# Neighbourhood attention regrouped into blocks of 8 grid columns, and narrower end tiles in the window attention

## The chip, the cores and the metric

One core of one Trainium2 chip runs the whole program. The metric is the time of one execution in device microseconds (us); lower is better. Three runs of the kernel before gave 2230.81, 2233.44 and 2235.84 us, so the median is 2233.44 us.

## What is computed

A backbone of two layers over 512 latent tokens (a grid of 8 rows by 64 columns) and 256 context tokens, 1,024 channels wide, all in fp32. In each layer the normalised tokens are projected to queries, keys and values of four attention branches with four heads each: A (latent attention, dense), B (window: a latent query sees latent keys at a distance of at most 128), C (neighbourhood) and D (normalised queries and keys, dense). Every latent query also sees all 256 context keys in the same softmax. The context tokens see context keys alone, and only layer 0 needs them. Each branch's output is projected, multiplied by a gate (a sigmoid of a product of the tokens with a 1,024 x 1,024 matrix per branch) and summed; then come an output projection and a mixture of 32 experts.

The part that matters here, cut from the reference (8 grid rows, so a query sees all rows):

```python
c_start = clip(q_col - NA_KW // 2, 0, GRID_W - NA_KW)      # NA_KW = 16, GRID_W = 64
col_ok = (k_col >= c_start) & (k_col < c_start + NA_KW)
dc = clip(k_col - q_col, -(NA_KW - 1), NA_KW - 1) + NA_KW - 1
bias = rpb[:, dr, dc]                                      # dr: row distance; 0 for context keys
s = where(row_ok & col_ok, q @ k * scale + bias, -1e30)
```

So of the 512 latent keys a query of branch C sees 16 columns of 8 rows, 128 keys, and the rest is masked.

## The kernel before, in words

Tokens are handled in six tiles of 128: 0 to 3 latent (each two grid rows), 4 and 5 context. fp32 values are split in a high and a low part in the fast fp32 format ("fp32r"), and a product is three products (`mm3`, L306); `projT` (L664) makes 128 channels by up to 512 tokens in one PSUM bank, so 24 matmuls, and `proj` (L657) one token tile by 256 channels, also 24.

`branch_c` (L829) works in two halves of two heads. `qk` (L833) projects queries and keys in `projT` form, 512 latent tokens and then 256 context tokens; `val` (L853) projects the values one token tile at a time. `bias_c` (L1106) loads a table of 128 x 896 for each head through the POOL queue and combines it with the column mask on DVE.

`attend` (L1071) cuts a half into groups of 256 queries, two of them latent, and a group into four tiles (two query tiles by two heads). `scores` (L1114) makes one tile: the products of 128 queries with the latent keys (512, in branch B 384) and the 256 context keys into a PSUM buffer of two banks (`sps`, two of these); DVE takes the row minimum of the context part and adds the bias or the mask to the latent part while taking the minimum on (L1135, L1142); ACT takes the exponential with its sum (L1152); DVE scales (L1156, L1157); then PE transposes P in pieces of 128 keys into banks (`bk`, four of these, L256) and ACT copies them to `pt` (L1169). `values` (L1091) multiplies `pt` with the values in plain fp32, both heads side by side in the array, copies the sum (L1101) and writes it to DRAM on the SP queue (L1102).

The order on PE is written out by a planner, `Flow` (L143): it keeps a clock from an estimate for each matmul (`mat`, L244) and fixed latencies (the tables `LT`, one per layer) for the time until a buffer is free again or a result is ready. Where the attention's items are not ready, it puts in a filler, `gates` (L1173): the 32 gate products of the layer, with the products of the modulation vector between them in layer 0 (`mod_seg`, L392), whose weights come through the SP queue (L403, L285). Whatever is left of the filler runs on into `merge` (L1205), which reads the branch outputs back from DRAM (`load`, L1220). The other engines take their orders from the framework's scheduler. Expert weights are loaded on the SP queue (L1644) as buffer slots come free.

Of the kernel before, what the change touches and what calls it, by code (L numbers as in the profile page):

```python
# [9 lines left out]
F32 = mybir.dt.float32  # L10
# [3 lines left out]
AF = mybir.ActivationFunctionType  # L14
ALU = mybir.AluOpType
# [8 lines left out]
NL = 2  # L24
# [3 lines left out]
BIG = 1e30  # L28
# [17 lines left out]
def consts():  # L46
    c = {}
    c["ident"] = np.eye(128, dtype=np.float32)
    c["rope_h"] = _rope(SEQ, 64)
    c["rope_a"] = _rope(SEQ, 32)  # L50
    a, b = np.arange(128)[:, None], np.arange(128)[None, :]
    full = np.full((128, 128), BIG, np.float32)
    zero = np.zeros((128, 128), np.float32)
    lo = np.where(b >= a, 0.0, BIG).astype(np.float32)
    hi = np.where(b <= a, 0.0, BIG).astype(np.float32)
    c["bmask"] = np.concatenate([full, lo, zero, hi, full], 1)
    qc = np.arange(128)[:, None] % 64
    kc = np.arange(64)[None, :]
    cs = np.clip(qc - 8, 0, 48)
    c["cmask"] = np.where((kc >= cs) & (kc < cs + 16), 0.0, BIG).astype(np.float32)  # L60
# [24 lines left out]
def prep(x, c, ctx, c_ctx, w_mod, b_mod, g_norm_mix, w_in, g_q_a, w_q_b, g_kv_a, w_kv_b,  # L85
         sink_b, rpb_c, g_q_d, g_k_d, w_gate, b_gate, w_branch, w_out, g_norm_ffn,
         w_group, b_group, w_router, b_router, w_ff1, w_ff3, w_ff2, g_final):
    r = {}
# [26 lines left out]
    pad = np.zeros((NL, 4, 15, 128), np.float32)  # L115
    pad[..., 48:79] = rpb_c
    qc, kc = np.arange(64)[:, None], np.arange(64)[None, :]
    sk = pad[..., kc - qc + 63]
    bt = np.stack([sk[:, :, 1:15], sk[:, :, 0:14]], 2)
# [113 lines left out]
class Build:  # L233
# [110 lines left out]
    def setup(self):  # L344
# [12 lines left out]
        def rest():  # L357
            self.rope_h = ld("rope_h", [128, 4, 2, 64])
            self.rope_a = ld("rope_a", [128, 4, 2, 32])
            self.bmask = ld("bmask", [128, 640])  # L360
            self.cmask = ld("cmask", [128, 64])
            self.iota = ld("iota", [128, 64])
            self.trib = c.tile([128, 128], BF, name="trib")

# [299 lines left out]
    def projT(self, W, c0, t0, n):  # L664

        ps = self.bank()
        c = slice(c0, c0 + 128)
        self.mm3(ps[:, :n], [(W(0, k)[:, c], W(1, k)[:, c], self.hsl(0, k, t0, n), self.hsl(1, k, t0, n))
                             for k in range(8)])
        return ps  # L670

    def nop(self, give=0, fn=None):
# [156 lines left out]
    def branch_c(self):  # L829
# [3 lines left out]
        def qk(hb, part, t0, n):  # L833
# [3 lines left out]
            for j in range(2):  # L837
                own, oth = slice(64 * j, 64 * j + 64), slice(64 - 64 * j, 128 - 64 * j)
                if part == 0:
                    q = hf.q(t0, n)  # L840
                    nc.scalar.activation(q[own, j], ps[own, :n], AF.Copy, scale=-0.125)
                    nc.vector.scalar_tensor_tensor(q[oth, j], ps[own, :n], -0.125, q.bitcast(F32)[own, j],
                                                   op0=ALU.mult, op1=ALU.subtract)
# [9 lines left out]
        def val(t):  # L853
# [4 lines left out]
            return  # L858
            yield

        vals = []
        for hb in range(2):
            load, new = self.load_unit(box, 4 + 2 * hb), self.new_half(box, hb, "m")
            bias = f.item(self.nop(0, lambda hb=hb: box.__setitem__(("bt", hb), [self.bias_c(2 * hb + j)
                                                                                for j in range(2)])), slots=2)
            pre = [load, new, bias]
            ps = []
            for t0, n in ((0, 512), (512, 256)):
# [11 lines left out]
            out.append((pre, proj, lambda hb=hb, ps=ps: self.attend("c", 2, hb, box, ps + vals, None), 7))  # L880
        return out

    def head_norm(self, s, H):
# [184 lines left out]
        return out  # L1068


    def attend(self, br, n, hb, box, qs, ks):  # L1071


        f = self.fl
        items = []
        for g in range(3 if self.wc else 2):
            kts = [4, 5]
            if g < 2:
                kts = list(range(g, g + 3) if br == "b" else range(4)) + kts
            groups = [kts[i:i + 3] for i in range(0, len(kts), 3)]  # L1080
            PT = [[], []]
            tiles = []
            for qi in range(2):
                deps = qs if ks is None else [qs[2 * g + qi]] + [ks[t] for t in kts]
                for j in range(2):
                    tiles.append(f.item(self.scores(br, hb, box, j, g, qi, groups, PT[j]), deps=deps, lat=self.LT["evac"],
                                        need=("S", "P")))
            items += tiles + [f.item(self.values(n, hb, box, g, kts, PT), deps=tiles, lat=self.LT["pv"], need=("bk",))]
        return items

    def values(self, n, hb, box, g, kts, PT):  # L1091
        f, hf = self.fl, box[hb]
        acc = self.bank()
        f.use("bk", self.LT["oacc"])
        for i, kt in enumerate(kts):
            for j in range(2):
                self.mat(acc[64 * j:64 * j + 64, :256], hf.v(j, kt), PT[j][i // 3][:, i % 3, :],
                         start=i == 0, stop=i == len(kts) - 1, tile_position=(0, 64 * j))
        f.left["pt1"] += len(PT[0]) + len(PT[1])
        oT = self.t1("oT")  # L1100
        self.nc.vector.tensor_copy(oT, acc[:, :256])  # L1101
        self.nc.sync.dma_start(self.ob[n][hb][:, g * 256:(g + 1) * 256], oT)  # L1102
        return
        yield

    def bias_c(self, h):  # L1106
        nc = self.nc
        bt = self.slot(name="bt")[:, :896].rearrange("p (u c) -> p u c", u=14)
        nc.gpsimd.dma_start(bt.rearrange("p u c -> p (u c)"), self.a["rpb"][self.l, h])
        nc.vector.scalar_tensor_tensor(bt, bt, -1.0, self.cmask[:, None, :].to_broadcast([128, 14, 64]),  # L1110
                                       op0=ALU.mult, op1=ALU.add)
        return bt

    def scores(self, br, hb, box, j, g, qi, groups, PT):  # L1114
# [5 lines left out]
        q0 = g * 256 + qi * 128  # L1120
# [3 lines left out]
        q = hf.q(q0, 128)[:, j]  # L1124
        for c0, cn, kk in ([(lo, kn, k0)] if lat else []) + [(512, 256, 512)]:
            self.mat(S[:, c0:c0 + cn], q, hf.kh(0, j, kk, cn), start=True, stop=False)
            self.mat(S[:, c0:c0 + cn], q, hf.kh(1, j, kk, cn), start=False, stop=br != "a")
            if br == "a":
                self.mat(S[:, c0:c0 + cn], hf.qr(q0, 128)[:, j], self.KR[:, kk:kk + cn], start=False, stop=True)
        m = self.tiny.tile([128, 1], F32, name="m", tag="m", bufs=4)  # L1130
        if br in "ad" or not lat:
            nc.vector.tensor_reduce(m, S[:, lo:768], axis=AX.X, op=ALU.min)  # L1132
        else:
            m0 = self.tiny.tile([128, 1], F32, name="m0", tag="m0", bufs=4)
            nc.vector.tensor_reduce(m0, S[:, 512:768], axis=AX.X, op=ALU.min)  # L1135
            if br == "b":
                o = {0: 2, 1: 1, 2: 1, 3: 0}[2 * g + qi]
                bias = self.bmask[:, o * 128:o * 128 + 384]
            else:
                u = 7 - 2 * (2 * g + qi) - 1  # L1140
                bias = box["bt", hb][j][:, u:u + 8].rearrange("p u c -> p (u c)")
# [18 lines left out]
        for gi, grp in enumerate(groups):  # L1160
            if gi:
                yield 0.0, ("bk",)
            elif qi == 0:
                PT += [self.sm.tile([128, 3, 256], F32, name="pt", tag="pt", bufs=NPT) for _ in groups]
                f.left["pt1"] -= len(groups)
            w = len(grp)
            f.use("bk", self.LT["pt"])
            v = self.transposed([Pt[:, (gi * 3 + i) * 128:(gi * 3 + i + 1) * 128] for i in range(w)])
            nc.scalar.activation(PT[gi][:, :w, qi * 128:(qi + 1) * 128], v, AF.Copy)  # L1169
        f.left["P"] += 1  # L1170


# [843 lines left out]
```

## Time and profile before

| | |
|---|---|
| median of 3 runs | 2233.44 us (2230.81 to 2235.84) |
| the profiled execution | 2233.74 us, span 2232.0 us |
| PE busy | 2068.5 us (93% of the span) |
| DVE, ACT, POOL busy | 1288.5, 808.8, 295.7 us |
| mean granted clock of PE | 0.965 |
| DMA | 430.92 MB, 193 GB/s on average |

PE is TensorE's matmuls and PEld its weight loads, DVE is VectorE, ACT ScalarE, POOL GpSimd and SP the engine that issues most DMAs. A row of the timeline gives start, duration and, after the shape, how many instructions were merged in it; matmuls overlap, so the distance from start to start says what one costs PE, not its duration. "L251" is the helper through which nearly every matmul goes, "L256" the one for transposes. A matmul in plain fp32 shows as two rows.

### The profile page before, as it was taken

The numbers are of one execution on the slowest core, as the hardware profiler recorded it, in microseconds if no ns is written. First come the engines' busy times: TensorE is split into PE (matmuls) and PEld (weight loads), VectorE is DVE, ScalarE is ACT, GpSimd is POOL, SyncE is SP. The second block draws the span as 40 slices with busy tenths as digits, with TensorE's granted clock in tenths as the row PEclk, the third lists the DMA queues.
The fourth block names the chain that finished last, engine by engine and source line by source line (L and its number), as shares of the span: only waits on it lengthen the run. The fifth ranks groups of instructions, "written<-read, shape, count | busy, mean of one in ns | idle before, by whom it ended". The sixth has DMA issues, their size and how long they took to land. (4 is left out here: it accounts for less than half of the span.)

```text
span 2232.0 us, 34108 instructions
## 1 busy us (share of the span) xinstructions
PE 2068.5 (93%) x13005; PEld 1524.7 (68%) x13005; DVE 1288.5 (58%) x2655; ACT 808.8 (36%) x1817; POOL 295.7 (13%) x321
## 2 busy tenths in 40 slices
PE   5999999999999988969999979999999998699997
PEld 3878777777887877934444468877888787644443
DVE  4464454345544565677777766555466476746655
ACT  4454454344444221212222235565455432211112
POOL 1101100011100144230000031000020013200000
PEclk8999999999999998979999989999999999899999
DMA  7452443543223555679999423112212387699992
GB/s 280 144 195 95 152 155 113 171 149 119 81 78 115 188 187 197 227 254 402 365 366 364 178 76 107 55 48 90 90 46 86 121 259 263 226 379 407 406 406 80
DMA packets 141813, 430.92 MB, mean 193 GB/s; under 512 B 19344, under 2 KB 32032, under 8 KB 141648
## 3 DMA queue, kind: packets, MB, share of 16 engines
q1 hardware_dynamic: 127120, 388.36, 48.4%
q0 software_dynamic: 13088, 35.10, 4.8%
q10 hardware_dynamic: 1440, 5.24, 0.6%
q8 instruction: 104, 1.70, 0.3%
q14 instruction: 61, 0.50, 0.1%
HBM read 398.67 MB, written 36.78 MB: 195 GB/s over the span
## 5 line engine op out<-in xcount | busy, mean ns | idle before, releaser
L251 PE MATMUL bk<-hT,wH 128*128 128x512 f32 (+1 forms) x1760 | 480.2, 360 | 2.8 <-ACT wH L275 2.1
L251 PEld LDWEIGHTS bk<-hT,wH 128*128 128x128 f32 x1760 | 300.1, 189 | 51.4 <-issue 8.1
L251 PE MATMUL bk<-hT,wL 128*128 128x512 f32 (+1 forms) x880 | 311.8, 354 | 7.6 <-DVE wL L276 7.6
L1786 DVE TENSOR_TENSOR x<-x,sps 128x1024 f32<-128x1024 f32 x166 | 195.5, 1216 | 101.0 <-PE sps L1785 100.6
L1727 PE MATMUL bk<-e,xT 128*64 128x512 f32 x1056 | 245.8, 603 | 0.0
L251 PE MATMUL bk<-wH,hT 128*128 128x256 f32 x1248 | 240.5, 287 | 1.3 <-DVE sk L276 1.0
L251 PEld LDWEIGHTS bk<-wH,hT 128*128 128x128 f32 x1248 | 200.0, 193 | 5.3 <-DVE sk L276 1.3
L251 PEld LDWEIGHTS bk<-hT,wL 128*128 128x128 f32 x880 | 166.3, 189 | 33.4 <-DVE wL L276 9.8
L275 ACT ACTIVATE wH<-wraw 128x1024 fp32r<-128x1024 f32 x132 | 139.1, 1058 | 125.1 <-DMA wraw<-in_w_gate_dram 41.5
L276 DVE TENSOR_TENSOR wL<-wraw,wH 128x1024 fp32r<-128x1024 f32 x112 | 138.8, 1245 | 70.2 <-ACT wH L275 39.4
L251 PE MATMUL bk<-wL,hT 128*128 128x256 f32 x624 | 177.2, 284 | 0.0
L1727 PEld LDWEIGHTS bk<-e,xT 128*64 128x64 f32 x1056 | 72.1, 138 | 142.9 <-issue 125.7
L1152 ACT ACTIVATE P<-sps,m 128x768 f32<-128x768 f32 (+2 forms) x160 | 126.5, 792 | 77.0 <-DVE m L1132 52.7
L1169 ACT ACTIVATE pt<-bk 128x384 f32<-128x384 f32 (+1 forms) x288 | 120.8, 467 | 74.7 <-PE bk L256 73.6
L1785 PE MATMUL sps<-yeH,to 128*128 128x512 f32 x332 | 142.7, 430 | 2.4 <-ACT yeH L275 1.4
L256 PE MATMUL bk<-ident,P 128*128 128x128 f32 x800 | 121.2, 282 | 19.2 <-ACT pt L1169 7.3
L1785 PE MATMUL sps<-yeL,to 128*128 128x512 f32 x332 | 132.2, 398 | 1.7 <-DVE yeL L276 1.7
L322 POOL TENSOR_TENSOR rr<-rs,mhalf 128x1 f32<-128x1 f32 (+1 forms) x72 | 52.3, 727 | 572.5 <-DVE rs L318 500.9
L1750 PE MATMUL bk<-e,gT 128*64 128x512 f32 x528 | 122.3, 606 | 1.5 <-ACT gT L1743 1.5
L256 PEld LDWEIGHTS bk<-ident,P 128*128 128x128 f32 x800 | 91.7, 142 | 46.7 <-ACT pt L1169 15.4
L251 PEld LDWEIGHTS bk<-wL,hT 128*128 128x128 f32 x624 | 120.3, 193 | 0.6
L1733 ACT ACTIVATE eth<-bk 128x256 f32<-128x256 f32 x33 | 12.7, 385 | 285.7 <-PE bk L1727 285.7
(355 smaller groups left out, 3671.4 us busy)
## 6 DMA issues: line engine op xcount, KB each, us to landing
e<-in_w_dram SPq DMA_DIRECT2D x384, 512.0 KB, 7.5
wmod<-in_w_mod_dram SPq DMA_DIRECT2D x96, 512.0 KB, 4.6
wraw<-in_w_gate_dram SPq DMA_DIRECT2D x64, 512.0 KB, 4.0
wraw<-in_w_in_dram SPq DMA_DIRECT2D x36, 512.0 KB, 4.9
thd<-th SPq DMA_DIRECT2D x64, 256.0 KB, 3.4
thm<-thd SPq DMA_DIRECT2D x32, 384.0 KB, 3.1
wraw<-in_w_br_dram SPq DMA_DIRECT2D x16, 512.0 KB, 4.0
wraw<-in_w_out_dram SPq DMA_DIRECT2D x16, 512.0 KB, 6.1
```

The lines of the kernel that those rows point to most:

```text
L251: return self.nc.tensor.matmul(out, lhsT, rhs, **kw)
L256: return self.nc.tensor.transpose(out, src, self.ident if ident is None else ident)
L275: nc.scalar.activation(H, src, AF.Copy)
L276: (eng or nc.vector).tensor_tensor(L, src, H.bitcast(F32), op=ALU.subtract)
L322: self.nc.gpsimd.tensor_tensor(r[:, :n], o[:, :n], self.mhalf.to_broadcast([128, n]), op=ALU.pow)
L1152: nc.scalar.activation(Pt[:, :n], S[:, lo:768], AF.Exp, scale=-1.0, bias=m, accum_out=sm)
L1169: nc.scalar.activation(PT[gi][:, :w, qi * 128:(qi + 1) * 128], v, AF.Copy)
L1727: nc.tensor.matmul(box["h"][64 * z:64 * z + 64, :], xT(k, z), W(z, k // 2)[:, (k % 2) * 512:(k % 2 + 1) * 512], start=k == 0, stop=k == 7, ...
L1733: nc.scalar.activation(th[s], H[s, :256], AF.Tanh, scale=0.5)
L1750: nc.tensor.matmul(Y[n][64 * z:64 * z + 64, :], gT[:, k, 64 * z:64 * z + 64], W(z, 4 + k)[:, n * 512:(n + 1) * 512], start=k == 0, stop=k ...
L1785: nc.tensor.matmul(ps[:, c], to[s, t * 128:(t + 1) * 128], w[s, c], start=i == 0, stop=i == 1)
L1786: nc.vector.tensor_tensor(self.x1[t] if out is None else out, self.x1[t], ps, op=ALU.add)
```

## The change

The 64 grid columns are cut into 8 blocks of 8; a block has 8 rows by 8 columns, 64 tokens. The q, k and v products of branch C's latent tokens are written to PSUM in block order (block, row, column) by a strided output pattern; the tokens are still read in their old order. The queries are copied out rotated by one block, so that the query tiles are blocks (1, 2), (3, 4), (5, 6) and (7, 0); the key tiles are blocks (0, 1), (2, 3), (4, 5), (6, 7). A query tile then sees two key tiles, 256 latent keys: tile u sees u and u + 1, the last one sees 0 and 3. The values of the latent tokens are projected as `projT` too (channels by tokens), copied and transposed back on PE. The bias with the mask in it comes as one table of 128 x 1,024 for a half (2 heads, 2 kinds of query tile, 256 keys) and is negated on ACT. In branch B the first and the last query tile see 256 latent keys in place of 384. `values` multiplies a key tile with the queries that see it alone, context tile 4 first and 5 last. The outputs of branch C are put back in grid order by four copies and written in pieces of 32, 24 or 8 columns.

```diff
 # prep
-    r["rpb"] = f(bt.transpose(0, 1, 2, 4, 3, 5).reshape(NL, 4, 128, 14 * 64))
+    for qb, kb in (((1, 2), (0, 1, 2, 3)), ((7, 0), (0, 1, 6, 7))):
...
+        tabs.append(np.where(ok, rpb_c[:, :, kr[None] - qr[:, None] + 7, dc], np.float32(-BIG)))
 # projT
+        out = ps[:, :n]
+        seen = lambda z, k: self.hsl(z, k, t0, n)
+        if t0 == 0:
+            seen = lambda z, k: self.hsl(z, k, t0, n).rearrange("p (r b c) -> p r b c", r=8, c=8)
+            out = out.rearrange("p (b r c) -> p r b c", r=8, c=8)
+        self.mm3(out, [(W(0, k)[:, c], W(1, k)[:, c], seen(0, k), seen(1, k)) for k in range(8)])
 # branch_c, qk
+                    for d, s, m in ((0, 64, 448), (448, 0, 64)) if t0 == 0 else ((0, 0, n),):
+                        d, s = slice(d, d + m), slice(s, s + m)
+                        nc.scalar.activation(q[own, j, d], ps[own, s], AF.Copy, scale=-0.125)
+                        nc.vector.scalar_tensor_tensor(q[oth, j, d], ps[own, s], -0.125, q.bitcast(F32)[own, j, d],
+                                                       op0=ALU.mult, op1=ALU.subtract)
 # branch_c
+        def valT(i):
+            ps = self.projT(box["u", 5], 128 * i, 0, 512)
+            f.use("bk", self.LT["cacc"])
+            vT = [self.t1("vT") for _ in range(2)]
+            for z in range(2):
+                nc.scalar.activation(vT[z], ps[:, 256 * z:256 * z + 256], AF.Copy)
+            yield self.LT["kt"], ("bk",)
+            v = self.transposed([vT[t // 2][:, t % 2 * 128:t % 2 * 128 + 128] for t in range(4)])
+            f.use("bk", self.LT["vacc"])
+            nc.scalar.activation(box[i].V[:, 0:4], v, AF.Copy)
...
-                vals = [f.item(val(t), deps=[lv, new, new1], lat=self.LT["load"], need=("bk",)) for t in range(6)]
+                vals = [f.item(v, deps=[lv, new, new1] + self.norms, lat=self.LT["load"], need=("bk",))
+                        for v in [valT(i) for i in range(2)] + [val(t) for t in (4, 5)]]
 # attend
+    def keys(self, br, u):
+        if br == "b":
+            return list(range(max(u - 1, 0), min(u + 2, 4)))
+        if br == "c":
+            return [u, u + 1] if u < 3 else [0, 3]
+        return list(range(4))
...
+            groups = [kts[:-2], [4, 5]] if len(kts) == 5 else [kts[i:i + 3] for i in range(0, len(kts), 3)]
 # values
+        at = at[-2:-1] + at[:-2] + at[-1:]
+        for gi, i, kt in at:
+            q = [qi for qi in range(2) if kt in see[qi]]
+            c = slice(128 * q[0], 128 * q[-1] + 128)
             for j in range(2):
+                self.mat(acc[64 * j:64 * j + 64, c], hf.v(j, kt), PT[j][gi][:, i, c],
+                         start=kt == 4, stop=kt == 5, tile_position=(0, 64 * j))
...
+        if br == "c" and g < 2:
+            rows = oT.rearrange("p (r b c) -> p r b c", r=8, b=4)
+            src = acc[:, :256].rearrange("p (b r c) -> p b r c", b=4, r=8)
+            for b in range(4):
+                nc.vector.tensor_copy(rows[:, :, b], src[:, b])
+            grid = out[:, :512].rearrange("p (r c) -> p r c", r=8)
+            for b, m, c0 in ((0, 4, 8),) if g == 0 else ((0, 3, 40), (3, 1, 0)):
+                nc.sync.dma_start(grid[:, :, c0:c0 + 8 * m], oT.rearrange("p (r x) -> p r x", r=8)[:, :, 8 * b:8 * b + 8 * m])
+            return
 # bias_c
+        bt = self.slot(name="bt")
+        self.nc.gpsimd.dma_start(bt, self.a["rpb"][self.l, hb])
+        self.nc.scalar.activation(bt, bt, AF.Copy, scale=-1.0)
 # scores
-        k0, kn = (g * 128, 384) if br == "b" else (0, 512)
-        lo = 512 - kn if lat else 512
+        kts = see[:-2]
+        kn = 128 * len(kts)
+        lo = 512 - kn
...
+            if wrap and k0 == 0:
+                out = out.rearrange("p (t n) -> p t n", t=2)
+                kk = lambda z: hf.kh(z, j, 0, 512).rearrange("p (t n) -> p t n", t=4)[:, 0:4:3]
...
+            v = self.transposed([Pt[:, see.index(grp[i]) * 128:see.index(grp[i]) * 128 + 128] for i in own])
+            nc.scalar.activation(PT[gi][:, i0:i0 + w, qi * 128:(qi + 1) * 128], v, AF.Copy)
```

The constant `cmask` and its load at the start go away, and a half of branch C takes one slot less for its bias.

## Rows read from the trace of the kernel before

**Rows 1.** The page, busy time of PE: us, share of the span, instructions.

```profile
PE 2068.5 (93%) x13005; PEld 1524.7 (68%) x13005; DVE 1288.5 (58%) x2655; ACT 808.8 (36%) x1817; POOL 295.7 (13%) x321
```

**Rows 2.** Stages of core 0: length, busy PE, PEld, DVE, ACT, POOL; clock, DMA share, GB/s.

```profile
60.00:700.00 640.00, 617.02 (x4460) 505.40 (x4459) 308.59 (x789) 299.27 (x747) 57.68 (x89) 0.99 0.38 128
430.00:560.00 130.00, 124.47 (x907) 100.02 (x910) 61.78 (x151) 56.18 (x129) 16.83 (x26) 0.99 0.38 129
1310.00:1800.00 490.00, 467.87 (x3007) 395.85 (x3006) 277.35 (x661) 252.52 (x608) 37.07 (x44) 0.99 0.25 81
1600.00:1720.00 120.00, 113.90 (x771) 95.79 (x770) 78.84 (x198) 61.66 (x148) 16.21 (x23) 1.00 0.17 55
```

**Rows 3.** PE's waits from 430 (first) and 1600 us (second): total us, times, longest.

```profile
PE bk L256 <- DVE P L1157: 2.7, 1, 2.7
...
PE bk L256 <- DVE oT L1101: 0.7, 1, 0.7
```

**Rows 4.** Timeline of the SP queue at the end of either attention: start us, duration us.

```profile
697.39 0.33 SPq L285 DMA_DIRECT2D wraw<-in_w_gate_dram  x1
...
1719.70 0.33 SPq L285 DMA_DIRECT2D wraw<-in_w_gate_dram  x1
```

**Rows 5.** Line 1644, the expert loads: ns min/median/max, first and last start us.

```profile
L1644 SPq DMA_DIRECT2D e<-in_w_dram x384: 327/330/1213, 888.4 to 2173.6; - x192
```

**Rows 6.** Timeline of PE, pieces that set the unit prices.

```profile
470.24 0.39 PE L251 MATMUL bk<-hT,wL 128*128 128x512 f32 x1
470.46 0.61 PE L251 MATMUL bk<-hT,wH 128*128 128x512 f32 x2
470.92 0.39 PE L251 MATMUL bk<-hT,wL 128*128 128x512 f32 x1
...
477.50 0.28 PE L251 MATMUL bk<-hT,wL 128*128 128x256 f32 x1
477.62 0.40 PE L251 MATMUL bk<-hT,wH 128*128 128x256 f32 x2
477.86 0.28 PE L251 MATMUL bk<-hT,wL 128*128 128x256 f32 x1
...
395.08 0.88 PE L256 MATMUL bk<-ident,P 128*128 128x128 f32 x6
395.71 0.36 PE L251 MATMUL sps<-sc 128*128 128x256 f32 x1
...
541.58 2.81 PE L251 MATMUL bk<-pt,V 128*64 128x256 f32 x24
544.32 0.64 PE L251 MATMUL bk<-wmod,silu 128*32 128x256 f32 x8
```

**Rows 7.** Timeline of PE's weight loads for the values products.

```profile
481.30 1.71 PEld L251 LDWEIGHTS bk<-pt,V 128*64 128x64 f32 x18
```

**Rows 8.** Groups by line and shape: count, busy us, mean ns, idle before.

```profile
L1727 PE MATMUL bk<-e,xT 128*64 128x512 f32 x1056 | 245.8, 603 | 0.0
...
L1101 DVE COPY oT<-bk 128x256 f32<-128x256 f32 x40 | 16.9, 423 | 45.6 <-PE bk L251 45.3
...
L690 DVE TENSOR_TENSOR r<-bk,rope_a 128x64 f32<-128x64 f32 x16 | 3.6, 223 | 5.8 <-ACT dup L714 5.7
...
L1169 ACT ACTIVATE pt<-bk 128x256 f32<-128x256 f32 x64 | 23.4, 383 | 20.9 <-PE bk L256 20.7
```

**Rows 9.** Tiles oT (output writes) and rcol (1,024 four-byte pieces): issue to landing.

```profile
DMA to landing us min/median/max: 1.7/1.7/5.4
...
DMA to landing us min/median/max: 7.1/8.7/11.2
```

**Rows 10.** Timeline of SP, then PE: the fourth w_mod load of a segment, and its product.

```profile
541.00 0.33 SPq L403 DMA_DIRECT2D wmod<-in_w_mod_dram  x1
...
552.18 0.64 PE L251 MATMUL bk<-wmod,silu 128*32 128x256 f32 x8
```

**Rows 11.** Tile wmod from 500 to 560 us: issue to landing.

```profile
DMA to landing us min/median/max: 4.4/4.4/4.4
```

More of the change, by code (lines that the diff above doesn't have):

```diff
@@ L863, in branch_c @@
             load, new = self.load_unit(box, 4 + 2 * hb), self.new_half(box, hb, "m")
-            bias = f.item(self.nop(0, lambda hb=hb: box.__setitem__(("bt", hb), [self.bias_c(2 * hb + j)
-                                                                                for j in range(2)])), slots=2)
+            bias = f.item(self.nop(0, lambda hb=hb: box.__setitem__(("bt", hb), self.bias_c(hb))), slots=1)
             pre = [load, new, bias]
@@ L1076, in attend @@
         for g in range(3 if self.wc else 2):
[L1077 to L1080, printed above, removed]
+            see = [self.keys(br, 2 * g + qi) + [4, 5] if g < 2 else [4, 5] for qi in range(2)]
+            kts = [t for t in see[0] if t < 4] + [t for t in see[1] if t < 4 and t not in see[0]] + [4, 5]
+            groups = [kts[:-2], [4, 5]] if len(kts) == 5 else [kts[i:i + 3] for i in range(0, len(kts), 3)]
             PT = [[], []]
@@ L1083, in attend @@
             for qi in range(2):
-                deps = qs if ks is None else [qs[2 * g + qi]] + [ks[t] for t in kts]
+                deps = qs if ks is None else [qs[2 * g + qi]] + [ks[t] for t in see[qi]]
                 for j in range(2):
-                    tiles.append(f.item(self.scores(br, hb, box, j, g, qi, groups, PT[j]), deps=deps, lat=self.LT["evac"],
-                                        need=("S", "P")))
-            items += tiles + [f.item(self.values(n, hb, box, g, kts, PT), deps=tiles, lat=self.LT["pv"], need=("bk",))]
@@ L1089, in attend, with values @@
-        return items
-    def values(self, n, hb, box, g, kts, PT):
-        f, hf = self.fl, box[hb]
+                    tiles.append(f.item(self.scores(br, hb, box, j, g, qi, see[qi], groups, PT[j]), deps=deps,
+                                        lat=self.LT["evac"], need=("S", "P")))
+            items += tiles + [f.item(self.values(br, n, hb, box, g, see, groups, PT), deps=tiles, lat=self.LT["pv"],
+                                     need=("bk",))]
+        return items
+    def values(self, br, n, hb, box, g, see, groups, PT):
+        f, hf, nc = self.fl, box[hb], self.nc
@@ L1099, in values @@
         f.left["pt1"] += len(PT[0]) + len(PT[1])
         oT = self.t1("oT")
[L1101 to L1102 removed]
+        out = self.ob[n][hb]
+        if br == "c" and g < 2:
[7 more added lines that the diff above has]
+            return
@@ L1103, in values @@
+        nc.vector.tensor_copy(oT, acc[:, :256])
+        nc.sync.dma_start(out[:, g * 256:(g + 1) * 256], oT)
         return
         yield
[L1106 to L1112, printed above, removed]
@@ L1114, in scores, with bias_c @@
-    def scores(self, br, hb, box, j, g, qi, groups, PT):
+    def bias_c(self, hb):
+        bt = self.slot(name="bt")
+        self.nc.gpsimd.dma_start(bt, self.a["rpb"][self.l, hb])
+        self.nc.scalar.activation(bt, bt, AF.Copy, scale=-1.0)
+        return bt.rearrange("p (j w k) -> p j w k", j=2, w=2)
+    def scores(self, br, hb, box, j, g, qi, see, groups, PT):
         nc, f, hf = self.nc, self.fl, box[hb]
         lat = g < 2
-        k0, kn = (g * 128, 384) if br == "b" else (0, 512)
-        lo = 512 - kn if lat else 512
-        q0 = g * 256 + qi * 128
+        u = 2 * g + qi
+        kts = see[:-2]
+        kn = 128 * len(kts)
+        lo = 512 - kn
@@ L1123, in scores @@
         f.left["P"] -= 1
[L1124 to L1127, printed above, removed]
+        wrap = br == "c" and u == 3
+        q = hf.q(u * 128, 128)[:, j]
+        for c0, cn, k0 in ([(lo, kn, 128 * kts[0])] if lat else []) + [(512, 256, 512)]:
+            out = S[:, c0:c0 + cn]
+            if wrap and k0 == 0:
+                out = out.rearrange("p (t n) -> p t n", t=2)
+                kk = lambda z: hf.kh(z, j, 0, 512).rearrange("p (t n) -> p t n", t=4)[:, 0:4:3]
+            else:
+                kk = lambda z: hf.kh(z, j, k0, cn)
+            self.mat(out, q, kk(0), start=True, stop=False)
+            self.mat(out, q, kk(1), start=False, stop=br != "a")
             if br == "a":
-                self.mat(S[:, c0:c0 + cn], hf.qr(q0, 128)[:, j], self.KR[:, kk:kk + cn], start=False, stop=True)
+                self.mat(out, hf.qr(u * 128, 128)[:, j], self.KR[:, k0:k0 + cn], start=False, stop=True)
         m = self.tiny.tile([128, 1], F32, name="m", tag="m", bufs=4)
@@ L1165, in scores @@
                 f.left["pt1"] -= len(groups)
-            w = len(grp)
+            own = [i for i, kt in enumerate(grp) if kt in see]
+            i0, w = own[0], len(own)
             f.use("bk", self.LT["pt"])
-            v = self.transposed([Pt[:, (gi * 3 + i) * 128:(gi * 3 + i + 1) * 128] for i in range(w)])
-            nc.scalar.activation(PT[gi][:, :w, qi * 128:(qi + 1) * 128], v, AF.Copy)
+            v = self.transposed([Pt[:, see.index(grp[i]) * 128:see.index(grp[i]) * 128 + 128] for i in own])
+            nc.scalar.activation(PT[gi][:, i0:i0 + w, qi * 128:(qi + 1) * 128], v, AF.Copy)
         f.left["P"] += 1
```

33 lines of the change are left out of this document (13 added, 20 removed).

## The prediction

> **What bounds the kernel now.** I read the profile's page first, then the stages, then who waits for whom. The page shows TensorE (PE) busy 93% of the span [rows 1]. The stages say where the change falls: the attention of layer 0 lies between 60 and 700 us and that of layer 1 between 1310 and 1800 us; PE is busy 617.0 of 640 us and 467.9 of 490 us there, at a granted clock of 0.99, the 2.4 GHz level, with DVE and ACT at about half and the DMA engines at 0.25 to 0.38 [rows 2]. So PE stands idle 23.0 + 22.1 = 45.1 us in both. While the neighbourhood branch is at work (430 to 560 us, 1600 to 1720 us) it is idle 5.5 and 6.1 us; the largest wait there is one of 2.7 us for a scaled P [rows 2, 3]. The gate products fill what the attention leaves open, and gate weights are still being loaded at 697 us and at 1719 us [rows 4], so this filler outlasts both neighbourhood stages. What is to be seen: in the stages that the change touches, time is PE work, and a microsecond of PE work taken out is nearly a microsecond of span. After them come the output projection and the experts; the expert weights move from 888 us on [rows 5], when the slots of the merge are given back, so that part should begin earlier by as much.
>
> **The unit prices**, from spacing on PE, not from a row's duration, since matmuls overlap: three 512-column products start within 0.68 us, so 0.227 us each; three 256-column ones within 0.36 us, so 0.120; one of 384 columns I put between them, at 0.174; six transposes take 0.63 us, so 0.105; a group of values products (12 products of 256 columns in plain fp32, 24 in the trace because each shows twice) 541.58 to 544.32 us, so 0.228 us each [rows 6].
>
> **What is taken out, per layer.**
> - Neighbourhood scores: 16 latent tiles (2 halves, 2 groups, 2 query tiles, 2 heads), each with two latent products of 256 columns in place of 512: 32 x 0.107 = 3.4 us.
> - Their transposes: 4 in place of 6 a tile: 32 x 0.105 = 3.4 us.
> - Their values: a group has 12 products of 256 columns; after, 6 of 256 and 4 of 128 (five key tiles, two of them seen by one query tile alone). No row has 128 columns in this form. Half of 0.228 is the lower end, 0.228 the upper; the weight loads, 18 within 1.71 us or 0.095 each with two to a product [rows 7], and half the columns at 0.114 leave it nearer the lower: I take 0.158. A group falls from 2.74 to 1.37 + 0.63 us; four groups save 3.0 us (1.8 to 3.6).
> - Window branch, 8 end tiles at 256 in place of 384 latent keys: 16 x 0.054 = 0.9 us of scores, 8 x 0.105 = 0.8 us of transposes; in each of 4 groups 2 of 10 values products halve: 8 x 0.07 = 0.6 us (0 to 0.9).
> - The v projection of the four latent tiles: 96 products of 256 columns become 48 of 512: 11.5 against 10.9 us, 0.6 us less; but 8 transposes come in, 0.8 us.
>
> That is 3.4 + 3.4 + 3.0 + 0.9 + 0.8 + 0.6 + 0.6 - 0.8 = 11.9 us a layer, 23.8 us in all (20.2 to 25.6 with the bounds of the values). DVE and ACT are relieved too, as the bias pass, the exponential, the scaling and the copies of P work on fewer columns; I count that at nothing, as PE hardly waits for them.
>
> **What is put in.**
> - The output copy of a group is 4 copies of 128x64 in place of one of 128x256: 4 x 0.223 against 0.423 us [rows 8], so its PSUM bank comes free 0.47 us later, 8 times. Behind it waits whoever wants one of the four banks; DVE's own queue is half empty. 0 to 3.8 us; I take 1.0, because a bank wait for this copy is seen once, at 0.7 us [rows 3].
> - The v transposes wait for two copies on ACT; the planner puts 1.3 us of other work between. Cover gone, it would be four times two copies of 0.383 us [rows 8], 3.1 us; I take 0.5.
> - The last query tile reads its keys as two runs of 128 in one product (16 of these): between nothing and the 0.107 us that its shortening gave, 1.7 us; I take 0, since the column count is what the spacing followed.
> - The negation of the bias moves from DVE (8 passes) to ACT (4), and each Q copy falls into two pieces; both run on engines that are half empty beside a busy PE [rows 2]: 0. If a bias load were late, ACT would hold the exponentials that are queued behind the negation, and PE would wait for P; but the load waits only for a slot and is asked for ahead of the projections. POOL issues 4 loads in place of 8. One small load less at the start: 0.
> - 12 output writes on the SP queue now have 1,024 pieces of 128, 96 or 32 bytes. An output write lands in 1.7 us; 1,024 tiny pieces (on POOL's queue) in 8.7 [rows 9]. The reader is the merge, behind the whole of branch D. Behind them in SP's queue wait w_mod and gate loads: the fourth w_mod load of a segment is issued at 541.00 us, its product starts at 552.18, landing takes 4.4 us [rows 10, 11], so some 7 us are spare. I take 0; the end without cover is the second rival.
> - The 288 projection products of 512 columns (96 for q and k, 48 for v, two layers) write PSUM in runs of 8 with a stride. Every matmul of the trace writes contiguous columns, so no row shows this. A gain is excluded: columns and clock stay. The lower end is 0; for the upper I take the slowest 512-column product there is, an expert product in plain fp32, 1056 rows in 245.8 us and two rows to a product, so 0.466 us [rows 8]: 288 x 0.239 = 69 us. I take 0: the nearest row is the same product with the same 512 columns and contiguous writes, spacing follows the columns (0.227 against 0.120), and runs of 8 keep neighbours together.
>
> The Trainium skill, PSUM: Partial Sum Buffer (Specifications), speaks against this: it gives PSUM 8-byte cachelines and says that any non-contiguous access pattern slows matmuls significantly. By its letter, with the upper end as the price, the sum would be +46 us; if only the cacheline counts, runs of 32 bytes waste none of it, and the sum stays as it is below. No row here shows either.
>
> The sum: -23.8 + 1.5 = -22.3 us. The profiled execution took 2233.74 us (span 2232.0, 1.7 around it), 0.3 above the median of 2233.44, so no correction: 2233.7 - 22.3 = **2211 us**. With the bounds (a gain of 20.2 less costs of 3.8 + 3.1 + 1.7 = 8.6 is 11.6; one of 25.6 with some of PE's waits gone is 27), this case's own range is 2206 to 2222.
>
> **The rivals.**
> 1. *Strided PSUM writes slow the projections.* Place: the runs of 24 products for q, k and v, which stand on PE itself with nothing beside them. Price 0 to 69 us; from 22.3 / 288 = 0.077 us a product (0.227 to 0.304) it eats the whole gain and decides the sign. At the upper end 2211 + 69 = 2280 us. For it: PE has no slack there. Against: same columns, neighbours kept. Chance 0.18. (The page of the Trainium skill named above is the rule behind this one.)
> 2. *The small output writes hold up SP's loads.* Each delays what is queued behind it by 7 us more; the second group of a half issues two, so 14 us against 7 spare: PE loses 7 us a half, in layer 0 alone 14 us: 2225; in both layers 28: 2239. For it: w_mod loads follow the writes directly in SP's queue. Against: the 8.7 us is another queue's. Chance 0.11. (The Trainium skill, DMA: Bandwidth & Descriptors, Specifications, puts the smallest transfer for line rate at 512 bytes; no row here shows such writes on SP.)
> 3. *The re-planned order opens gaps.* PE's order is made by a planner with fixed latencies, which nobody refits; the work becomes shorter but its due times don't. If PE's 45.1 us of idling grew by half, the gain would be gone: about 2234. Against: the filler isn't used up. Chance 0.05.
>
> That the narrowing doesn't happen can be left out: products, transposes and softmax all take their width from the same list of seen tiles.
>
> **The numbers.** My forecast has 0.66. A measurement of this kernel tells about 0.2%, 4.5 us, from no change. Faster (below 2229): 0.66 and 0.07 of rival 2 make 0.73. Same: 0.01 of rival 1, 0.03 of rival 2, 0.04 of rival 3, 0.08. Slower: 0.17, 0.01 and 0.01, 0.19. The range 2206 to 2238 holds the forecast's own range and nearly all of rivals 2 and 3; left out are rival 1 above its break-even and the tails.
>
> **What would show it.** In the changed profile: 512-column projection products that write the neighbourhood's banks still 0.227 us apart (0.3 or more: rival 1); 40 transposes of P fewer a layer and 8 of v more; values groups at about 2.0 us; PE idle in the two attentions near 45 us (clearly more: rival 3, and if the releaser is a w_mod or gate load, rival 2); the first expert load some 11 us earlier in layer 0. The forecast is wrong if PE's work falls by 24 us and the span doesn't, or if PE's work doesn't fall.

## The result, and the profile after

The changed kernel takes **2210.58 us** (median of 4 runs, 2208.86 to 2211.77) against 2232.12 us (2228.95 to 2235.84) for the kernel before beside it: a ratio of 0.990, with a 95% interval of 0.988 to 0.992. The forecast was 2211 us. The profiled execution took 2210.27 us, with a span of 2208.5 us, 23.5 us less than before.

The page of the changed kernel, busy time of each engine, answers to [rows 1]:

```profile
PE 2040.4 (92%) x12813; PEld 1500.6 (68%) x12813; DVE 1266.5 (57%) x2679; ACT 799.9 (36%) x1825; POOL 291.9 (13%) x317
```

PE is busy 28.1 us less and the span is 23.5 us shorter, so the span followed PE, though not one for one: a part of the 28.1 us is time at a lower clock, as will be seen. For the two layers I cut each trace at the same events: layer 0 from 60 us, layer 1 from the load of its tokens, both to the first product of the output projection. What lies outside these stages takes 884.1 us before and 885.1 us after, so the gain is inside them. Stages of the kernel before (length, busy PE, PEld, DVE, ACT, POOL; clock, DMA share, GB/s; they hold what [rows 2] hold and the merge behind it):

```profile
60.00:835.40 775.40, 742.32 (x5156) 611.39 (x5155) 381.35 (x878) 331.54 (x794) 94.16 (x117) 0.98 0.41 138
1287.30:1859.80 572.50, 542.86 (x3351) 457.79 (x3351) 338.94 (x740) 281.43 (x649) 67.77 (x68) 0.98 0.32 104
```

The same stages of the changed kernel:

```profile
60.00:815.40 755.40, 726.86 (x5072) 599.05 (x5072) 371.72 (x895) 328.83 (x804) 90.81 (x115) 0.99 0.43 142
1267.60:1835.60 568.00, 532.47 (x3254) 447.89 (x3255) 328.69 (x752) 277.53 (x653) 67.21 (x66) 0.98 0.32 103
```

Layer 0 is 20.0 us shorter, layer 1 only 4.5; PE's busy time falls by 15.5 and 10.4. Those numbers don't look like 11.9 us twice. Two things are mixed into them: idle time, and busy time at a lower granted clock. To part them I read both stages in windows of 2 us and summed busy time times granted clock (the work, in microseconds at the full clock) and busy time times what is missing to 1.00 (the loss). A second profiled execution of the changed kernel (the one in E9) gives 719.8 and 525.5 us of work where this one gives 722.3 and 525.8, so a sum is good to some 2.5 us.

```text
                      layer 0                            layer 1
                span   work  loss  idle          span   work  loss  idle
before         775.4  733.0   9.3  33.1         572.5  537.6   5.2  29.6
after          755.4  722.3   4.6  28.5         568.0  525.8   6.7  35.5
difference     -20.0  -10.7  -4.7  -4.6          -4.5  -11.8  +1.5  +5.9
```

**The work fell by 10.7 and 11.8 us, where 11.9 was forecast for each layer** (13.2 and 12.1 by the second execution). The uneven shift of the two ends is waits and the clock behind them: 9.3 us came on top in layer 0, 7.4 us were lost again in layer 1. The trace shows how a wait and the clock hang together. Windows of the kernel before around its wait of 2.7 us for a scaled P, the one of [rows 3]:

```profile
500.00:502.00 2.00, 0.00 (x0) 0.00 (x0) 2.00 (x4) 1.64 (x2) 2.00 (x3) 1.00 0.70 285
502.00:504.00 2.00, 1.40 (x7) 1.43 (x8) 2.00 (x5) 1.15 (x4) 2.00 (x3) 0.63 0.00 0
504.00:506.00 2.00, 2.00 (x15) 0.86 (x15) 1.88 (x5) 1.49 (x5) 0.58 (x2) 0.51 0.01 4
506.00:508.00 2.00, 2.00 (x20) 1.33 (x22) 1.57 (x3) 0.90 (x1) 0.00 (x0) 1.00 0.37 96
```

PE stood idle for 2.7 us, and the granted clock of the next 4 us is 0.63 and 0.51, near the lower level of 1.2 GHz: 1.40 x 0.37 + 2.00 x 0.49 = 1.5 us more. The wait cost 4.2 us. In the changed kernel it is gone. A larger wait of layer 0 is gone with it, one of 4.95 us for the low part of a gate weight; PE's timeline of the kernel before, and the windows from there on:

```profile
674.34 0.79 PE L251 MATMUL bk<-hT,wL 128*128 128x512 f32 x1 [4.95 <-DVE wL L276]
```

```profile
674.00:676.00 2.00, 1.66 (x5) 1.38 (x5) 1.94 (x3) 0.60 (x2) 0.00 (x0) 0.50 0.47 176
676.00:678.00 2.00, 2.00 (x11) 2.00 (x11) 0.96 (x1) 0.77 (x2) 0.00 (x0) 0.50 0.75 262
678.00:680.00 2.00, 2.00 (x9) 1.80 (x8) 0.00 (x0) 1.70 (x4) 0.00 (x0) 0.50 0.05 21
```

Here the loss is 1.66 x 0.50 + 2.00 x 0.50 + 2.00 x 0.50 = 2.8 us, so this wait cost 7.8 us. The changed kernel has two shorter ones of the kind in its place, 2.38 us at 655 us and 2.04 us at 725 us, the first with a loss of 1.7 us behind it, the second with none.

In layer 1 it went the other way: waits for the low part of a gate weight came up (and those for a copy of P grew, from 4.5 to 7.2 us). PE's waits in layer 1 (who, for whom: total us, times, longest), first the kernel before:

```profile
PE bk L251 <- DVE wL L276: 1.2, 2, 0.7
```

and the changed one:

```profile
PE bk L254 <- DVE wL L279: 7.0, 4, 3.2
```

The longest, on PE's timeline of the changed kernel, with the windows from there on:

```profile
1772.83 0.80 PE L254 MATMUL bk<-hT,wL 128*128 128x512 f32 x1 [3.18 <-DVE wL L279]
```

```profile
1772.00:1774.00 2.00, 1.18 (x3) 0.98 (x4) 0.77 (x1) 0.00 (x0) 0.00 (x0) 0.67 0.92 270
1774.00:1776.00 2.00, 2.00 (x7) 1.52 (x6) 0.00 (x0) 1.09 (x2) 0.00 (x0) 0.50 0.36 141
1776.00:1778.00 2.00, 2.00 (x10) 1.66 (x9) 1.75 (x3) 0.92 (x1) 0.00 (x0) 0.98 0.00 0
```

**The unit prices after.** The last of the 24 products of a Q projection of the neighbourhood branch, which write PSUM in runs of 8 (it is one of those because ACT then copies 448 of its columns), on the timeline of the changed kernel, PE and then ACT:

```profile
353.92 0.61 PE L254 MATMUL bk<-hT,wH 128*128 128x512 f32 x2
354.37 0.39 PE L254 MATMUL bk<-hT,wL 128*128 128x512 f32 x1
354.60 0.82 PE L259 MATMUL bk<-ident,P 128*128 128x128 f32 x6
...
354.80 0.54 ACT L849 ACTIVATE sq<-bk 64x448 fp32r<-64x448 f32 x1 [4.64 <-PE bk L254]
```

Three products in 0.68 us: 0.227 each, to the third decimal what [rows 6] show with contiguous writes. The values group, and what follows it, on PE's timeline:

```profile
463.82 1.95 PE L254 MATMUL bk<-pt,V 128*64 128x256 f32 x20
465.71 0.72 PE L254 MATMUL bk<-hT,wH 128*128 128x512 f32 x2
```

It takes 1.89 us, with 10 products (20 rows). Six of 256 columns at 0.228 are 1.37, so the four of 128 columns cost 0.13 us each. The transposes of P, by shape, in the kernel before:

```profile
L256 PE MATMUL bk<-ident,P 128*128 128x128 f32 x800 | 121.2, 282 | 19.2 <-ACT pt L1169 7.3 <-ACT V L790 4.5 <-DVE P L1157 3.7
```

The counts by shape and the expert loads, as in [rows 8] and [rows 5], for the changed kernel:

```profile
L259 PE MATMUL bk<-ident,P 128*128 128x128 f32 x720 | 111.9, 280 | 15.6 <-ACT pt L1218 10.0 <-DVE P L1205 1.8 <-DVE oT L1143 0.7
...
L254 PE MATMUL bk<-pt,V 128*64 128x128 f32 x96 | 9.3, 273 | 0.0
...
L1138 DVE COPY oT<-bk 128x64 f32<-128x64 f32 x32 | 5.1, 215 | 3.1 <-PE bk L254 2.9
```

```profile
L1693 SPq DMA_DIRECT2D e<-in_w_dram x384: 327/328/1907, 868.2 to 2150.3; - x192
```

Transposes of P are 80 fewer in the two layers (720 in place of 800); the 16 of v are there too. The experts' weights start 20.2 us earlier than in [rows 5].

### The profile page after: what moved, and what is told of

The parts are those of the page before. It is cut to its first block, busy times and chain, and to the rows that moved or that the text cites. A ratio compares the mean times of both kernels' runs of the same rounds, so it can differ in the third digit from the quotient of the medians.

```text
span 2208.5 us, 33743 instructions
## 1 busy us (share of the span) xinstructions
PE 2040.4 (92%) x12813; PEld 1500.6 (68%) x12813; DVE 1266.5 (57%) x2679; ACT 799.9 (36%) x1825; POOL 291.9 (13%) x317
## 5 line engine op out<-in xcount | busy, mean ns | idle before, releaser
L254 PE MATMUL bk<-hT,wH 128*128 128x512 f32 (+1 forms) x1824 | 499.6, 361 | 2.6 <-ACT wH L278 2.1
L254 PEld LDWEIGHTS bk<-hT,wH 128*128 128x128 f32 x1824 | 312.4, 189 | 52.8 <-issue 8.9
L254 PE MATMUL bk<-hT,wL 128*128 128x512 f32 (+1 forms) x912 | 324.6, 356 | 11.9 <-DVE wL L279 11.9
L254 PE MATMUL bk<-wH,hT 128*128 128x256 f32 x1120 | 218.3, 288 | 2.7 <-ACT V L796 1.3
L254 PEld LDWEIGHTS bk<-wH,hT 128*128 128x128 f32 x1120 | 180.3, 193 | 6.0 <-ACT V L796 1.6
L254 PE MATMUL bk<-wL,hT 128*128 128x256 f32 x560 | 159.1, 284 | 0.0
L1200 ACT ACTIVATE P<-sps,m 128x768 f32<-128x768 f32 (+3 forms) x160 | 117.7, 736 | 54.8 <-DVE m L1181 38.3
L259 PE MATMUL bk<-ident,P 128*128 128x128 f32 x720 | 111.9, 280 | 15.6 <-ACT pt L1218 10.0
L1181 DVE TENSOR_REDUCE m<-sps 128x1 f32<-128x768 f32 (+1 forms) x96 | 73.7, 776 | 72.0 <-PE sps L254 71.4
L259 PEld LDWEIGHTS bk<-ident,P 128*128 128x128 f32 x720 | 81.8, 141 | 45.1 <-ACT pt L1218 19.6
```

What stands on the lines that cost most here:

```text
L254: return self.nc.tensor.matmul(out, lhsT, rhs, **kw)
L259: return self.nc.tensor.transpose(out, src, self.ident if ident is None else ident)
L1200: nc.scalar.activation(Pt[:, :n], S[:, lo:768], AF.Exp, scale=-1.0, bias=m, accum_out=sm)
```

## The experiments

The theory: in these stages time is PE's work; that work falls by 24 us, and nothing that the change puts in lies on PE's path. The rivals are those of the prediction.

**E1, the window branch alone.** The kernel before takes over the new `attend`, `values` and `scores`, but the neighbourhood branch keeps its 512 keys and its old order. In the function that lists the key tiles a query tile sees, it differs from the changed kernel by this:

```diff
         if br == "c":
-            return [u, u + 1] if u < 3 else [0, 3]
+            return list(range(4))
```

> The kernel before with the window branch's two end tiles narrowed to 256 latent keys and nothing else. If time follows the PE work taken out: 2 layers x (0.9 + 0.8 + 0.6) us = 4.6 us less than the kernel before, a ratio of about 0.998. If the re-planned order counts for more than the work: anything within 6 us of the kernel before on either side, since layer 1 of the changed kernel idled 6 us more.

Measured: 2227.31 us, ratio 0.997 (0.9953 to 0.9987). **E2, the neighbourhood branch alone**: the changed kernel, with 384 keys for every window tile again:

```diff
         if br == "b":
-            return list(range(max(u - 1, 0), min(u + 2, 4)))
+            return list(range(u // 2, u // 2 + 3))
```

> The changed kernel with the window branch's end tiles wide again (384 keys). If time follows the PE work: 4.6 us more than the changed kernel, so some 17 to 18 us less than the kernel before (ratio about 0.992). If the order counts for more: off that by up to 6 us.

Measured: 2211.51 us, ratio 0.9913 (0.9888 to 0.9937). The parts add up within the intervals: 0.30% and 0.87% are 1.17%, the whole is 1.0%. By far most of the gain is the neighbourhood's; E2's ratio lies 0.0014 above the changed kernel's, 3 us where 4.6 were expected, and their intervals overlap. The work at the full clock, summed as above, gives it part by part:

```text
                        layer 0                            layer 1
                  span   work  loss  idle          span   work  loss  idle
E1 (window)      765.9  731.5   4.6  29.8         581.0  534.7   9.5  36.8
E2 (neighb.)     763.0  723.2   8.0  31.8         563.9  526.6   6.3  31.1
```

From the kernel before to E1 the window branch takes 1.5 and 2.9 us out (2.3 forecast); from E2 to the changed kernel it is 0.9 and 0.8, so its share is known no better than the sums are. The neighbourhood takes out 9.8 and 11.0 (9.6 forecast). But E1's layer 1 is 8.5 us longer than before with less work in it: its order brings 7.2 us of idle time and 4.3 us of loss. The span of one layer says little about a change of a few microseconds.

**E3, the small output writes twice** (rival 2: do they hold up SP's loads?):

```diff
+                for _ in range(2):
+                    nc.sync.dma_start(grid[:, :, c0:c0 + 8 * m], oT.rearrange("p (r x) -> p r x", r=8)[:, :, 8 * b:8 * b + 8 * m])
-                nc.sync.dma_start(grid[:, :, c0:c0 + 8 * m], oT.rearrange("p (r x) -> p r x", r=8)[:, :, 8 * b:8 * b + 8 * m])
```

> The changed kernel with every one of its 12 small-piece output writes issued twice. If they are hidden: the changed kernel's time within 3 us, with 24 such writes of about 0.38 us each on the SP queue. If they hold up the loads behind them in that queue: 14 to 28 us slower than the changed kernel.

Measured: 2208.02 us (2206.07 to 2211.93), ratio 0.9896 (0.987 to 0.9922). The writes on the SP queue of this kernel (ns min/median/max of the issue, first and last start, and then us from issue to landing), the ordinary ones and the small ones:

```profile
L1145 SPq DMA_DIRECT2D o<-oT x32: 319/326/944, 118.9 to 1738.4; - x32
...
DMA to landing us min/median/max: 1.7/1.7/5.5
...
L1142 SPq DMA_DIRECT2D o<-oT x24: 359/377/574, 462.5 to 1646.4; - x24
...
DMA to landing us min/median/max: 2.1/3.2/4.7
```

A small write holds the queue for 377 ns where an ordinary one takes 326; it lands in 3.2 us, against 1.7 for an ordinary one and the 8.7 that the rival took over from POOL's queue. Twelve more of them cost nothing that can be measured. PE's waits for a w_mod load, the sign that was named for rival 2, are 4.6 us in all in the changed kernel (9 times, the longest 1.2) against 3.1 before, but they all lie ahead of 460 us and the first small write starts at 466.5, so they don't come from the writes. Rival 2 falls. The Trainium skill, DMA: Bandwidth & Descriptors (Specifications), puts the smallest transfer for line rate at 512 bytes. The trace agrees in so far as the small writes land later, 3.2 us against 1.7; that costs nothing here, as nobody waits for them.

**E4 and E5, strided PSUM writes in many more products** (rival 1). All 1,536 products of 512 columns of the gates write in block order too, in runs of 8 columns, and the tanh reads them back in grid order; in E5 the runs are of 2 columns (`c=2`):

```diff
+                        o, v = G[:, :tn], y
+                        if t0 == 0:
+                            o, v = o.rearrange("p (b r c) -> p r b c", r=8, c=8), y.rearrange("p (r b c) -> p r b c", r=8, c=8)
-                        self.mat(G[:, :tn], x[:, k], y, start=k == 0 and y is a and x is H,
+                        self.mat(o, x[:, k], v, start=k == 0 and y is a and x is H,
...
-                nc.scalar.activation(th[:, :tn], G[:, :tn], AF.Tanh, scale=0.5, bias=hb[:, n, m:m + 1])
+                dst, src = th[:, :tn], G[:, :tn]
+                if t0 == 0:
+                    dst, src = dst.rearrange("p (r b c) -> p r b c", r=8, c=8), src.rearrange("p (b r c) -> p r b c", r=8, c=8)
+                nc.scalar.activation(dst, src, AF.Tanh, scale=0.5, bias=hb[:, n, m:m + 1])
```

> The changed kernel with the 1536 gate products of 512 columns also written to PSUM in runs of 8 with a stride, and read back in order by the tanh. If such writes are free: the changed kernel's time within 3 us and products still 0.227 us apart. If they cost anything that the 288 of the change hid: five times as much in addition, so 10 ns a product give 15 us and the break-even price of 77 ns gives 118 us.

> As the run with gate products in runs of 8, but in runs of 2 neighbouring columns. If strided PSUM writes are free as long as neighbours come in pairs: the changed kernel's time within 3 us, products 0.227 us apart. If any non-contiguous pattern costs and runs of 8 only made it small: four times as many runs in each of 1536 products, so 10 ns more a product shows as 15 us.

Measured: 2207.76 us (ratio 0.9891, 0.9866 to 0.9915) and 2208.7 us (0.9893, 0.9866 to 0.9919). PE's timeline of E4, gate products in runs of 8 and then a contiguous product:

```profile
702.02 0.62 PE L254 MATMUL bk<-hT,wH 128*128 128x512 f32 x2
702.48 0.39 PE L254 MATMUL bk<-hT,wL 128*128 128x512 f32 x1
702.71 0.61 PE L254 MATMUL sps<-oHL,wH 128*128 128x512 f32 x2
```

and PE's timeline of E5, the same place in runs of 2:

```profile
702.00 0.63 PE L254 MATMUL bk<-hT,wH 128*128 128x512 f32 x2
702.47 0.39 PE L254 MATMUL bk<-hT,wL 128*128 128x512 f32 x1
702.70 0.62 PE L254 MATMUL sps<-oHL,wH 128*128 128x512 f32 x2
```

0.69 and 0.70 us for three products, 0.230 and 0.233 each. The work of both layers, in which 3 ns more a product would be 4.6 us, is 1,245.4 us in E4 and 1,247.7 in E5, against 1,248.1 and 1,245.3 in the two executions of the changed kernel. At the break-even price of rival 1, 0.077 us a product, 1,536 of them would have cost 118 us.

**E6, runs of a single column.** All values products but the neighbourhood's own, 304 in plain fp32 (the 296 of the expectation and 8 for context queries of the neighbourhood branch), write columns that lie 32 bytes apart, and two copies put them back:

```diff
+                o, v = acc[64 * j:64 * j + 64, c], PT[j][gi][:, i, c]
+                if not (br == "c" and g < 2):
+                    o = o.rearrange("p (t b r) -> p t r b", r=8, b=16)
+                    v = v.rearrange("p (t r b) -> p t r b", r=8, b=16)
-                self.mat(acc[64 * j:64 * j + 64, c], hf.v(j, kt), PT[j][gi][:, i, c],
+                self.mat(o, hf.v(j, kt), v,
...
```

> The changed kernel with the values products of branches A, B and D (296 products in plain fp32, 0.228 us for 256 columns) writing single columns 32 bytes apart, and two strided output copies in place of one. If single strided columns are free in plain fp32: the changed kernel's time within 3 us. If each column costs a whole write of its own: up to twice 0.228 us, some 60 us slower.

Measured: 2211.98 us, ratio 0.9914 (0.9889 to 0.9938), its median 1.4 us above the changed kernel's. A window group of ten products takes 2.10 us there,

```profile
171.41 2.17 PE L254 MATMUL bk<-pt,V 128*64 128x256 f32 x20
173.51 0.50 PE L254 MATMUL sps<-sk,sq 128*128 128x256 f32 x2
```

and 2.09 us in the changed kernel:

```profile
173.45 2.17 PE L254 MATMUL bk<-pt,V 128*64 128x256 f32 x20
175.54 0.50 PE L254 MATMUL sps<-sk,sq 128*128 128x256 f32 x2
```

Rival 1 falls, in all three forms. The rule of the Trainium skill, PSUM — Partial Sum Buffer (Specifications), that any non-contiguous access pattern slows matmuls significantly, is not borne out for these products: the measured spacing decides.

**E7 and E8, another order with the same work** (rival 3). Only the planner's share of filler in layer 1 differs:

```diff
-FILL = (0.8, 0.4)
+FILL = (0.8, 0.2)
```

> The changed kernel with the planner's share of filler in layer 1 at 0.2 in place of 0.4: the same work in another order on PE. If the order counts for little beside the work: within 4 us of the changed kernel, and layer 1's idle PE time (39.8 us there, 33.4 before) moves by no more. If the 6 us of idling that layer 1 gained come from the order alone, some orders should give them back: 4 to 6 us faster.

and with 0.6:

> The same with the share at 0.6: more filler early in layer 1, less left for the merge. Within 4 us of the changed kernel if the order counts for little; 4 to 6 us faster or slower if it is what moved layer 1.

Measured: 2215.66 us (2209.31 to 2216.05; ratio 0.9928, 0.9905 to 0.9951) and 2217.78 us (2207.02 to 2222.36; 0.9925, 0.9899 to 0.995). Both medians lie further off than the 4 us and neither is faster, but both intervals overlap the changed kernel's, 0.988 to 0.992. The idle times of layer 1 that the expectation names, 39.8 and 33.4 us, are 35.5 and 29.6 by the cut used here.

```text
                        layer 0                            layer 1
                  span   work  loss  idle          span   work  loss  idle
share 0.2        751.1  721.8   3.1  26.2         572.6  525.2   7.1  40.3
share 0.4, again 752.6  719.8   2.6  30.1         568.8  525.5   8.7  34.6
share 0.6        750.5  719.9   2.4  28.1         589.9  526.4  12.3  51.2
```

Layer 0 has the same code in all three. In layer 1 the work agrees within 1.2 us, and the span differs by 21. PE's waits in layer 1 at a share of 0.6:

```profile
PE sps L254 <- DVE thm L1298: 18.4, 10, 3.6
```

With more gates spent early, the merge has none left to put between its own products (after 1790 us no gate product follows, where the changed kernel still has some at 1810) and waits ten times for a gate's factor. So rival 3's mechanism exists: the profiled execution lost a good part of the gain to a bad order. It is the slowest of E8's six, whose fastest took 2207.02 us, so what the order costs on average is not shown. With the share of 0.4 the gain stayed.

**E9, the low parts of the gate weights on POOL.** Four of the changed kernel's waits of over 2 us are for the low part `wL` of a gate weight (10.2 us; all its waits for low parts make 11.9), so I tried whether DVE's queue, in which these low parts stand behind other work, is what is late there; the changed kernel ran once more beside it.

```diff
-GE = False
+GE = 1
```

> The changed kernel once more, beside the next one on the same chip: 2210 us (2207 to 2213). Both theories expect the work of PE at the full clock to be the same as before by the microsecond (some 722 us in layer 0 up to the first output projection product, 526 us in layer 1); what differs from run to run is then the clock alone, by 2 us.

> The low parts of the 64 gate weights are made on POOL instead of DVE. In the changed kernel PE waits four times 2.0 to 3.2 us for such a low part from DVE, 10.2 us in all, and the granted clock reads 0.5 to 0.67 for the 2 to 4 us after three of them. Theory that DVE's queue is what is late (the low parts stand behind the row minima and the scaling of P there): these waits go, with the clock lost after them, and POOL, busy 13%, takes 64 x 2.4 us = 154 us more: 2200 us (2196 to 2206). Rival, the weights themselves land late, or POOL's 2.4 us in place of 1.2 makes each low part later than the queue did: the waits stay or grow, 2210 to 2216 us. PE's work at the full clock is the same in both.

Measured: the changed kernel again 2209.5 us (2205.23 to 2210.68; ratio 0.9891, 0.9872 to 0.9909), this version **2223.14 us** (2218.77 to 2227.78; 0.9954, 0.9938 to 0.9969). That is slower than either theory expected. Of the four waits that the expectation counts in the changed kernel only two, those at 655 and 1772 us, have the lower clock behind them, not three. PE's waits for gate weights' low parts in this version from 60 us to the end of layer 1's stage,

```profile
PE bk L254 <- POOL wL L279: 14.5, 9, 2.6
```

and of the changed kernel:

```profile
PE bk L254 <- DVE wL L279: 11.9, 7, 3.2
```

The waits followed to POOL and became more, so moving the low parts there is no remedy. Whether DVE's queue is late is another question, and this run does not answer it, since a subtraction takes 2.4 us on POOL and 1.2 on DVE. The timelines of one such wait in the changed kernel, DVE and then PE,

```profile
1707.40 0.61 DVE L1205 TENSOR_SCALAR P<-P,rc 128x768 f32<-128x768 f32 x1
1707.92 1.21 DVE L279 TENSOR_TENSOR wL<-wraw,wH 128x1024 fp32r<-128x1024 f32 x1
...
1709.19 0.50 PE L254 MATMUL bk<-hT,wL 128*128 128x512 f32 x1 [2.62 <-DVE wL L279]
```

and of one in this version, POOL and then PE:

```profile
1709.25 2.36 POOL L279 TENSOR_TENSOR wL<-wraw,wH 128x1024 fp32r<-128x1024 f32 x1 [5.24 <-PE bk L254]
...
1711.66 0.50 PE L254 MATMUL bk<-hT,wL 128*128 128x512 f32 x1 [1.95 <-POOL wL L279]
```

On DVE the low part stands right behind the scaling of P, as the theory had it. POOL has no such queue: before each of the seven waits of over 1.6 us it had been idle, until ACT had the high part (three times), PE was through with earlier products (three, as here) or DVE with another low part (once), and then PE waited for the subtraction itself, 2.4 us (once 3.0). So the slower engine's own time may hide what the missing queue saved. The waits for low parts account for 2.6 of the 14 us; the rest of the loss stays open. No version that I ran beats the changed kernel beyond the intervals.

## Why the prediction was right, point by point

- **The bound.** Right: the work at the full clock fell by 22.5 us (10.7 + 11.8; 25.3 by the second execution) against 23.8, and the span by 23.5. That is as near as the windows can tell it.
- **Scores and transposes.** Right by the counts (80 transposes of P fewer) and by the spacing. The last query tile's keys in two runs were taken at 0, and that holds: after 30 of the neighbourhood's 32 second score products of 256 columns, those that the timeline parts, the next product starts 0.11 or 0.12 us later, the last tile's among them.
- **Values of 128 columns.** Taken at 0.158 us, measured 0.13; a group of the neighbourhood falls to 1.89 us (2.00 forecast). The term was 3.0 a layer and is 4 x (2.74 - 1.89) = 3.4.
- **Output copies.** Taken at 1.0 us (0 to 3.8). A copy of 128x64 takes 0.215 us, so four end 0.44 us later, but PE waits for an output copy once, 0.7 us, as before [rows 3]: nothing was added.
- **v transposes.** Taken at 0.5 us. Among PE's waits none is for the two copies (`vT`): 0.
- **Strided writes and small writes at 0.** Right, E3 to E6.
- **DVE's and ACT's relief at nothing.** Not quite: the 2.7 us wait for a scaled P in [rows 3] is gone, with the 1.5 us of clock behind it. It is not shown that the narrower softmax is what removed it: the wait at this place went in E1 too, where the neighbourhood's tiles are as wide as before, and E1 has one of 3.96 us for a scaled P at another, 671 us. The order alone can move such a wait.
- **Where it was wrong: the step that made an equal shift of each layer's end out of its work.** "The first expert load some 11 us earlier in layer 0" came out at 20.2 us, and layer 1 gave only 4.5. The step left out that the order around a stage is dealt anew, that waits of 2 to 5 us come and go with it, and that a wait can have a price in clock besides. In the sum of both layers the waits and the clock took 1.9 us off (idle +1.3, loss -3.2), so the total came out right. That they nearly cancelled is luck: E7 and E8 have the same work, and their medians are 5 and 7 us higher. Rival 3 named a mechanism that exists: E8's profiled execution, with a span of 2220.6 us, lost half the gain by it, so the range needed its upper part.

## What to carry to other kernels

Where PE is busy 93% of the time, price a change in products, from spacing on PE, and check it afterwards in busy time times granted clock, not in the shift of one stage's end. Expect a planner that deals the order anew to move some 5 us either way in a stage, and look for the waits over 2 us first, since their price is the wait and, often, the clock behind it. Where a layout has to be changed anyway, a strided write of TensorE's products to PSUM is worth a trial: here it cost nothing.

## What the runs showed of the hardware that was not expected

- A 512-column fp32r product costs 0.227 to 0.233 us whether it writes PSUM contiguously, in runs of 8 columns or of 2; plain fp32 products that write single columns 32 bytes apart keep their 2.1 us for ten.
- Writes to DRAM in 1,024 pieces of 32 to 128 bytes on the SP queue hold it for 377 ns and land in 3.2 us (E3, where each is issued twice), against 326 ns and 1.7 us for an ordinary output write.
- After some waits of PE the granted clock is near the lower level for about 4 us: 0.63 and 0.51 behind the 2.7 us wait at 502 us in the kernel before, 0.67 and 0.50 behind the 3.2 us wait at 1772 us in the changed one. Not after all: the changed kernel's wait of 2.6 us at 1709 us is followed by 1.00 in every window. Nor is it the place in the program: in two executions of the changed kernel the same wait, 2.38 and 2.37 us, is followed by 0.63 and 0.52 in one and by 1.00 throughout in the other. What sets them apart, no run here shows. In the two layers together such losses are 14.5 us before and 11.3 after.
